# A two-layer encoder trunk on one core: the banks of a value projection, the order of the wide pools, and the last squares and output queues changed

## The chip, the cores and the metric

The kernel runs on one core of a Trainium2 chip. The metric is the device time of one execution in microseconds (us); of three runs of the kernel before, the median is 2415.16 us (2414.27 to 2418.61). The profile is of one more execution. TensorE (PE; PEld is its weight load) multiplies, VectorE (DVE) and ScalarE (ACT) do elementwise work, GpSimd (POOL) small copies and stores, and SyncE (SP) issues most DMAs. Each engine works through its own instructions in the order in which they were put there. TensorE writes to PSUM, eight banks of 128 x 512 float32.

## The reference

One sequence of 1024 frames, 1024 channels, two layers. Layer 0 projects the normed input to an RWKV-7 group and an attention group; layer 1 is a convolution module. Each layer is followed by a squared-ReLU MLP, and a last RMSNorm gives the output.

```
x = x + mixer(rmsnorm(x, g0))                      # layer 0
    p_rwkv, q, k, v = split(h @ w_in)              # 8 heads x 64 of each group
    y = concat(rwkv7(p_rwkv), band_attention(q, k, v)) @ w_out
x = x + square(relu(rmsnorm(x, g1) @ up0)) @ dn0
x = x + conformer_conv(rmsnorm(x, g2))             # pw1, GLU, width-31 conv, LayerNorm, silu, pw2
x = x + square(relu(rmsnorm(x, g3) @ up1)) @ dn1
out = rmsnorm(x, gf)
```

The RWKV-7 group keeps a 64 x 64 state for each head and updates it frame by frame. In attention each chunk of 64 frames sees itself and the eight chunks before it.

## The kernel before, in words

The 1024 frames are worked on as two halves of 512 (h = 0 and 1); activations lie as eight tiles of 128 channels x 512 frames. Each dense product is made of three passes at reduced precision: the float32 operands are split into a high and a low part (`split` for activations, `weight_part`, L258 and L259, for weights: ACT casts the high part `wh`, DVE subtracts it to get the low part `wl`), and `dense` (L144) multiplies high by high, low by high and high by low. `gemm` runs over output tiles, loads the weights for each (L250, on SP's queue, four raw buffers `wr`), sums over eight k in a PSUM bank, and hands the bank to an `evac` function.

The first part of the program has these banks: d=2 for dense work, w=2, v=1 and c=1 for the recurrence, a=2 for attention. It projects half 0 (`w_in_gemm(0)`), then runs `rwkv(0)` and `attention(0)` while `w_in_gemm(1)` projects half 1, then `rwkv(1)` and `attention(1)` beside the output projection (`mixer_out(0)`, which reads the results of recurrence and attention, yd) and the MLP of half 0. Priorities set the order: instructions of the recurrence come before those of attention, and these before dense ones, which are put where nothing else is ready; dense matmuls come in runs (6 or 12) that are not broken up.

At the end of `w_in_gemm` the value projection (L422 to L437) computes V with frames on partitions: four banks, one for each 128 frames, all four fed by the same weight part for each k. There are four buffers for split weights here (pool wp1). The four banks are d, d, a, a (`SPARE`), for both halves. ACT scales each bank by the frames' norm factor and POOL's queue stores it to vd, which attention loads.

The recurrence uses w for its products, v to transpose and invert (L676, L688, L705), and c (`keep["cb"]`, L449) for the chain over chunks and the end of a unit (L736 to L784). Attention uses its two a banks for scores (L861, L863), transposed probabilities (L883) and the output product (visit helper, L160).

From L1159 on the program is in its wide part: five d banks, two output tiles at a time, eight split weight buffers. Its pools take the memory that the first part's pools (LoRA weights, wp1, middle tiles mp, recurrence, attention) give back: wp2 (weights), mp2 (middle tiles), sx, and up (conv weights dwt, halo, conv tiles), each above the one before. A tile in memory used earlier waits until the earlier tiles there are read.

At the very end the last MLP of half 1 adds its down projection to x (L913). Its last two output tiles are computed in two column halves of 256 frames. For each tile ACT squares x (L220), DVE adds the square to the sum `acc` (L221), ACT scales by gf (L1053), TensorE transposes (L1059) and ACT and DVE copy the result to output tiles (L1065, L1067). After the last tile of a column half, `write` sums `acc` over channels by a product with ones (L1079), takes the root and the reciprocal (L1082, L1083), scales four output tiles (ACT two, DVE two) and issues their four DMAs on SP (L1092).

Of the kernel before, what the change touches and what calls it, by code (L numbers as in the profile page):

```python
# [11 lines left out]
ALU = mybir.AluOpType  # L12
# [52 lines left out]
def encoder_trunk(ctx: ExitStack, tc: tile.TileContext, x, vecs, consts, ext, w2a2, g2, w_in, w_out,  # L65
# [108 lines left out]
    def boost():  # L174
        return At("support")
# [224 lines left out]
    def w_in_gemm(h, rhs, st, first=()):  # L400
        def evac(m, q, cols):
            rstd = st.rstd()
            s = tmp("t1")
            if Q0 <= m < K0:
                nc.vector.scalar_tensor_tensor(out=s[:], in0=q[:], scalar=0.125, in1=rstd[:],
                                               op0=ALU.mult, op1=ALU.mult)
            else:
                nc.vector.tensor_tensor(out=s[:], in0=q[:], in1=rstd[:], op=ALU.mult)  # L408
            ts = slice(h * T, (h + 1) * T)
            if Q0 <= m < V0:  # L410
                hi = tmp("t2")
                nc.scalar.copy(hi[:].bitcast(F32R), s[:])
                nc.vector.tensor_tensor(out=s[:].bitcast(F32R), in0=s[:], in1=hi[:], op=ALU.subtract)
                nc.gpsimd.dma_start(ph[m][:, ts], hi[:])
                stored[h, m] = nc.gpsimd.dma_start(pl[m][:, ts], s[:])
            else:
                stored[h, m] = nc.gpsimd.dma_start(pd[m][:, ts], s[:])

        run_of(RUN[0])
        gemm(w_in, 0, IN_ORDER, rhs, evac, st, first, mark=h)  # L420
        run_of(RUN[2])
        qs = [psum(tag) for tag in SPARE]  # L422
        for k in range(KT):
            with boost():
                hi, lo = (a[:].rearrange("p a b -> p (a b)")
                          for a in weight_part(w_in[k * P : (k + 1) * P, V0 * P : V0 * P + RW], RW))
            xh, xl = rhs[k]
            for t, q in enumerate(qs):
                ts = slice(t * P, (t + 1) * P)
                dense(q[:], xh[:, ts], hi, start=(k == 0), stop=False)  # L430
                dense(q[:], xl[:, ts], hi, start=False, stop=False)
                dense(q[:], xh[:, ts], lo, start=False, stop=(k == KT - 1))
        with boost():
            for t, q in enumerate(qs):
                s = tmp("t1")
                nc.scalar.activation(s[:], q[:], AF.Copy, scale=st.part[1][:, t : t + 1])
                nc.gpsimd.dma_start(vd[h * T + t * P : h * T + (t + 1) * P, :], s[:])  # L437
# [481 lines left out]

        gemm(w, row0, range(KT), rhs, evac, taper=taper, after=after, halves=halves)  # L920

    def norm_collect(xs, gname):
        st = Stat()
        rhs = [None] * KT

        def last(m, cols):
            if gname is not None:
                rhs[m] = split(xs[m][:], m, v(gname, m))
            st.add(xs[m][:], cols)

        return st, rhs, last

# [9 lines left out]
        return nrhs, st  # L942

    def ffn(xs, rhs, rst, up, dn, mp, nxt, out_to=None, late=None):
        st, nrhs, last = norm_collect(xs, nxt)
        if out_to is not None:
            out_to.st = st
        groups = DFF // D
        mids = [[None] * KT for _ in range(groups)]
        ahead = 2 if wide[0] else 0  # L950

        def evac(m, q, cols):
            rstd = rst.rstd()
            t = tmp("t1")
            nc.vector.scalar_tensor_tensor(out=t[:], in0=q[:], scalar=0.0, in1=rstd[:], op0=ALU.max, op1=ALU.mult)  # L955
            sq = tmp("t2")
            nc.scalar.activation(sq[:], t[:], AF.Square)  # L957
            hi = mp.tile([P, T], F32R, tag="mh", name="mh")
            nc.scalar.activation(hi[:], t[:], AF.Square)  # L959
            lo = mp.tile([P, T], F32R, tag="ml", name="ml")  # L960
            nc.vector.tensor_tensor(out=lo[:], in0=sq[:], in1=hi[:].bitcast(F32), op=ALU.subtract)  # L961
            mids[m // KT][m % KT] = (hi, lo)

        done = 0
        for grp in range(groups):
            end = grp == groups - 1
            if late is not None and end:
                with At("mixer"):
                    late()
            upto = min((grp + 1) * KT + ahead, DFF // P)  # L970
            gemm(up, 0, range(done, upto), rhs, evac, rst)
            done = upto
            residual_gemm(dn, grp * D, mids[grp], xs, last=last if end else None, taper=end and nxt is None,
                          after=out_to.add if end and out_to is not None else None,
                          halves=out_to is not None and out_to.final)
        return nrhs, st
# [68 lines left out]
    class Out:  # L1045
# [5 lines left out]
        def add(self, m, cols):  # L1051
            n = tmp("t1")
            nc.scalar.activation(n[:, cols], self.xs[m][:, cols], AF.Copy, scale=v("gf", m))  # L1053
            q = psum("o")
            c2, j = divmod(m, 4)
            ts = range(cols.start // P, cols.stop // P)
            for t in ts:
                with At("dense"):
                    nc.tensor.transpose(q[:, t * P : (t + 1) * P], n[:, t * P : (t + 1) * P], ident)  # L1059
            for t in ts:  # L1060
                if self.o[4 * c2 + t] is None:
                    self.o[4 * c2 + t] = self.op.tile([P, T + TAPS - 1], F32, tag="u", name="u", bufs=8)
                dst, src = self.o[4 * c2 + t][:, j * P : (j + 1) * P], q[:, t * P : (t + 1) * P]
                if t % 2:
                    nc.vector.tensor_copy(dst, src)  # L1065
                else:
                    nc.scalar.copy(dst, src)  # L1067
            if self.final and m == KT - 1:
                self.write(ts)

        def finish(self):
            with boost():
                self.write(range(4))

        def write(self, ts):
            q = psum("o")
            for t in ts:
                with At("dense"):
                    nc.tensor.matmul(q[:, t : t + 1], self.st.acc[:, t * P : (t + 1) * P], ones[:, 0:1], start=True, stop=True)  # L1079
            w = slice(ts[0], ts[-1] + 1)  # L1080
            r = self.r
            nc.scalar.activation(r[:, w], q[:, w], AF.Sqrt, bias=kc[:, 0:1], scale=1.0 / D)  # L1082
            nc.vector.reciprocal(out=r[:, w], in_=r[:, w])  # L1083
            for c2 in range(2):
                for t in ts:
                    rows = slice(self.h * T + t * P, self.h * T + (t + 1) * P)
                    o = self.o[4 * c2 + t][:, 0:T]
                    if t % 2:
                        nc.scalar.activation(o, o, AF.Copy, scale=r[:, t : t + 1])
                    else:  # L1090
                        nc.vector.tensor_scalar(o, o, r[:, t : t + 1], None, op0=ALU.mult)
                    nc.sync.dma_start(out[rows, c2 * T : (c2 + 1) * T], o)  # L1092


    with banks(d=2, w=2, v=1, c=1, a=2), tc.tile_pool(name="lop", bufs=1) as lop, tc.tile_pool(name="wp1", bufs=4) as wb[0]:
# [62 lines left out]

    wide[0] = True  # L1159
    run_of(1)  # L1160
    with banks(d=5, w=1, o=2), tc.tile_pool(name="wp2", bufs=8, reuse_waits="tile") as wb[0], tc.tile_pool(name="mp2", bufs=10, reuse_waits="tile") as mp, tc.tile_pool(name="sx", bufs=4, reuse_waits="tile") as extra[0], tc.tile_pool(name="up", bufs=1, reuse_waits="tile") as up:
        dwt = up.tile([P, KT * TAPS], F32, tag="dwt", name="dwt")
        nc.scalar.dma_start(dwt[:], vecs[:, VOFF["dw"] : NVEC])
        halo = up.tile([P, KT, TAPS - 1], F32, tag="halo", name="halo")
        nc.gpsimd.memset(halo[:], 0.0)
        us = glu(0, r, s, up)
        with At("mixer"):
            ca, sca = conv(us, up)
        with boost():
            xb = fetch_x(1)  # L1170
        r, s = mixer_out(1, xb, mp)
        r, s = ffn(xb, r, s, up0, dn0, mp, "g2", late=lambda: conv_norm(ca, sca, up))
        stash_x(1, xb)
        us = glu(1, r, s, up)
        with boost():
            xa = fetch_x(0)
        r, s = pw2_block(ca, xa)
        with At("mixer"):
            cb, scb = conv(us, up)
        o = Out(0, xa, up, False)  # L1180
        ffn(xa, r, s, up1, dn1, mp, None, o, late=lambda: conv_norm(cb, scb, up))
        deferred.append(o.finish)
        with boost():
            xb = fetch_x(1)
        r, s = pw2_block(cb, xb)
        ffn(xb, r, s, up1, dn1, mp, None, Out(1, xb, up, True))
        deferred.pop()()
# [69 lines left out]
```

## Time and profile before

| | us |
|---|---|
| median of three runs | 2415.16 |
| profiled execution | 2409.59 |
| its span, first to last instruction | 2407.5 |
| TensorE busy | 2374.8 |
| DVE busy | 1706.2 |
| ACT busy | 1198.9 |
| POOL busy | 117.1 |

A row of the timeline has the start in us, the duration in us, engine, line, operation, output tile <- input tiles, shapes and a count of merged instructions; in brackets stands how long the engine was idle before it and which work ended that wait. A row for a stretch has its bounds, its length, the busy time of PE, PEld, DVE, ACT and POOL with their instruction counts, the granted TensorE clock as a share of full speed, the share of the 16 DMA engines that was busy, and GB/s. Matmuls overlap: one shows 0.39 us, but they start about 0.23 us apart.

### The profile page before, as it was taken

The numbers are of one execution on the slowest core, as the hardware profiler recorded it, in microseconds if no ns is written. First come the engines' busy times: TensorE is split into PE (matmuls) and PEld (weight loads), VectorE is DVE, ScalarE is ACT, GpSimd is POOL, SyncE is SP. The second block draws the span as 40 slices with busy tenths as digits, with TensorE's granted clock in tenths as the row PEclk, the third lists the DMA queues.
The fourth block names the chain that finished last, engine by engine and source line by source line (L and its number), as shares of the span: only waits on it lengthen the run. The fifth ranks groups of instructions, "written<-read, shape, count | busy, mean of one in ns | idle before, by whom it ended". The sixth has DMA issues, their size and how long they took to land.

```text
span 2407.5 us, 37122 instructions
## 1 busy us (share of the span) xinstructions
PE 2374.8 (99%) x12804; PEld 1956.4 (81%) x12804; DVE 1706.2 (71%) x3575; ACT 1198.9 (50%) x2323; POOL 117.1 (5%) x243
## 2 busy tenths in 40 slices
PE   9999999899999999999999999999999999999998
PEld 7777777788888888888888888888888888888887
DVE  6787776587777764579999746799997465434434
ACT  6567666677676753434433335334333365423324
POOL 1120111100000000011000000000000000000000
PEclk9999999999999999999999999999999999999999
DMA  8574445633343323453333334433333334333332
GB/s 260 163 217 139 120 121 171 188 102 115 93 120 110 90 74 90 145 166 92 101 97 97 97 97 135 123 94 97 96 98 99 95 112 140 97 97 97 97 98 67
DMA packets 476042, 283.34 MB, mean 118 GB/s; under 512 B 44512, under 2 KB 453216, under 8 KB 475856
## 3 DMA queue, kind: packets, MB, share of 16 engines
q1 hardware_dynamic: 464976, 249.46, 35.7%
q0 software_dynamic: 9488, 30.28, 3.6%
q8 instruction: 101, 1.65, 0.3%
q10 hardware_dynamic: 1392, 1.24, 0.2%
q14 instruction: 85, 0.70, 0.1%
HBM read 247.31 MB, written 36.72 MB: 118 GB/s over the span
## 4 chain that ended last, share of the span: by engine, by line
PE 88%; DVE 4%; DMA 3%; ACT 3%; issue 1%; SPq 1%; ACTq 0%; DVEq 0%
PE d L144 77%; DMA pt<-pd 1%; PE a L160 1%; PE v L688 1%; PE a L883 1%; DVE wl L259 1%; PE a L144 1%; ACT wh L258 1%; PE a L861 1%; PE a L863 1%; PE c L746 1%; PE c L740 0%; DVE pr L650 0%; PE c L736 0%; PE v L676 0%
## 5 line engine op out<-in xcount | busy, mean ns | idle before, releaser
L258 ACT CAST wh<-wr 128x512 fp32r<-128x512 f32 x744 | 460.1, 620 | 922.9 <-PE d L144 839.0
L144 PE MATMUL d<-xh,wh 128*128 128x512 f32 x1872 | 745.6, 398 | 0.3 <-DVE t L408 0.2
L144 PE MATMUL d<-xh,wl 128*128 128x512 f32 x1872 | 730.7, 391 | 0.9 <-DVE wl L259 0.9
L144 PE MATMUL d<-xl,wh 128*128 128x512 f32 x1872 | 730.2, 390 | 0.0
L259 DVE TENSOR_TENSOR wl<-wr,wh 128x512 fp32r<-128x512 f32 x744 | 503.4, 687 | 197.5 <-ACT wh L258 142.2
L144 PEld LDWEIGHTS d<-xh,wl 128*128 128x128 f32 x1872 | 351.7, 188 | 76.4 <-DVE wl L259 1.3
L144 PEld LDWEIGHTS d<-xh,wh 128*128 128x128 f32 x1872 | 352.2, 188 | 70.0 <-issue 1.2
L144 PEld LDWEIGHTS d<-xl,wh 128*128 128x128 f32 x1872 | 352.3, 188 | 67.7 <-issue 0.5
L144 PE MATMUL d<-mh,wh 128*128 128x512 f32 (+1 forms) x1040 | 405.8, 390 | 0.0
L144 PE MATMUL d<-mh,wl 128*128 128x512 f32 (+1 forms) x1040 | 401.8, 386 | 0.0
L144 PE MATMUL d<-ml,wh 128*128 128x512 f32 (+1 forms) x1040 | 401.6, 386 | 0.0
L1014 DVE SCALAR_TENSOR_TENSOR cv<-u,dwt,cv 128x512 f32<-128x512 f32 x480 | 332.7, 749 | 0.7
L144 PEld LDWEIGHTS d<-mh,wl 128*128 128x128 f32 x1040 | 195.4, 188 | 40.0
L144 PEld LDWEIGHTS d<-ml,wh 128*128 128x128 f32 x1040 | 195.6, 188 | 37.6
L144 PEld LDWEIGHTS d<-mh,wh 128*128 128x128 f32 x1040 | 195.5, 188 | 37.7
L913 DVE TENSOR_TENSOR x<-d,x 128x512 f32<-128x512 f32 (+1 forms) x146 | 97.8, 681 | 152.1 <-PE d L144 151.6
L955 DVE SCALAR_TENSOR_TENSOR t<-d,rstd 128x512 f32<-128x512 f32 x128 | 86.6, 688 | 114.6 <-PE d L144 111.9
L961 DVE TENSOR_TENSOR ml<-t,mh 128x512 fp32r<-128x512 f32 x128 | 87.9, 689 | 12.6 <-ACT mh L959 9.5
L957 ACT ACTIVATE t<-t 128x512 f32<-128x512 f32 x128 | 80.0, 625 | 12.2 <-DVE t L955 11.2
L959 ACT ACTIVATE mh<-t 128x512 fp32r<-128x512 f32 x128 | 78.9, 616 | 0.0
L745 ACT ACTIVATE sd<-vs,dc 64x64 f32<-64x64 f32 x128 | 44.1, 345 | 40.7 <-DVE vs L749 29.6
L221 DVE TENSOR_TENSOR acc<-acc,t 128x512 f32<-128x512 f32 (+1 forms) x86 | 58.0, 675 | 8.4 <-ACT t L220 8.3
(271 smaller groups left out, 2335.0 us busy)
## 6 DMA issues: line engine op xcount, KB each, us to landing
wr<-in_up_dram SPq DMA_DIRECT2D x256, 256.0 KB
wr<-in_dn_dram SPq DMA_DIRECT2D x256, 256.0 KB
wr<-in_w_in_dram SPq DMA_DIRECT2D x103, 256.0 KB
wr<-in_pw_dram SPq DMA_DIRECT2D x96, 256.0 KB
wr<-in_w_out_dram SPq DMA_DIRECT2D x32, 256.0 KB
pd<-t POOLq DMA_DIRECT2D x28, 256.0 KB, 2.6
x<-xd SPq DMA_DIRECT2D x24, 256.0 KB
pt<-pd SPq DMA_DIRECT2D x42, 128.5 KB
```

The source lines that it names most:

```text
L144: ins = nc.tensor.matmul(*a, **k)
L160: ins = issue(*a, **k)
L221: nc.vector.tensor_tensor(out=self.acc[:, cols], in0=self.acc[:, cols], in1=sq[:, cols], op=ALU.add)
L258: nc.scalar.copy(hi[:], raw[:])
L259: nc.vector.tensor_tensor(out=lo[:], in0=raw[:], in1=hi[:].bitcast(F32), op=ALU.subtract)
L745: nc.scalar.activation(sd[hs[hd], :], sv[hs[hd], hd, c, :], AF.Copy, scale=dc[hs[hd], c : c + 1])
L913: nc.vector.tensor_tensor(out=xs[m][:, cols], in0=q[:, cols], in1=xs[m][:, cols], op=ALU.add)
L955: nc.vector.scalar_tensor_tensor(out=t[:], in0=q[:], scalar=0.0, in1=rstd[:], op0=ALU.max, op1=ALU.mult)
L957: nc.scalar.activation(sq[:], t[:], AF.Square)
L959: nc.scalar.activation(hi[:], t[:], AF.Square)
L961: nc.vector.tensor_tensor(out=lo[:], in0=sq[:], in1=hi[:].bitcast(F32), op=ALU.subtract)
L1014: nc.vector.scalar_tensor_tensor(out=c[:], in0=u[:, tap : tap + T], scalar=dw(tap), in1=c[:], op0=ALU.mult, op1=ALU.add)
```

## The change

Three edits. The value projection of half 1 takes the banks d, d, v, c; half 0's stays. The pools of the wide part are opened in the order up, mp2, sx, wp2. At the end of half 1, the squares of the last tile are computed by DVE and not added to `acc`: the product with ones sums `acc` and the squares in one PSUM group (twice as many small matmuls) and stands ahead of the last transposes. There ACT scales one of the four output tiles in place of two, and the second and third DMA of each column half are issued on ACT's queue. The output of half 0 keeps its way, in a function cut in two.

```
-        qs = [psum(tag) for tag in SPARE]
+        qs = [psum(tag) for tag in (SPARE if h == 0 else ("d", "d", "v", "c"))]
...
-    def norm_collect(xs, gname):
+    def norm_collect(xs, gname, final=False):
...
-            st.add(xs[m][:], cols)
+            if final and m == KT - 1:
+                sq = tmp("t2")
+                nc.vector.tensor_tensor(out=sq[:, cols], in0=xs[m][:, cols], in1=xs[m][:, cols], op=ALU.mult)
+                st.rest = sq
+            else:
+                st.add(xs[m][:], cols)
...
-        st, nrhs, last = norm_collect(xs, nxt)
+        st, nrhs, last = norm_collect(xs, nxt, out_to is not None and out_to.final)
...
-            q = psum("o")
             c2, j = divmod(m, 4)
             ts = range(cols.start // P, cols.stop // P)
+            if self.final and m == KT - 1:
+                self.sums([self.st.acc, self.st.rest], ts)
+            q = psum("o")
...
+        def sums(self, parts, ts):
             q = psum("o")
+            pairs = [(part, t) for part in parts for t in ts]
+            for i, (part, t) in enumerate(pairs):
                 with At("dense"):
+                    nc.tensor.matmul(q[:, t : t + 1], part[:, t * P : (t + 1) * P], ones[:, 0:1],
+                                     start=(i == 0), stop=(i == len(pairs) - 1))
             w = slice(ts[0], ts[-1] + 1)
             r = self.r
             nc.scalar.activation(r[:, w], q[:, w], AF.Sqrt, bias=kc[:, 0:1], scale=1.0 / D)
             nc.vector.reciprocal(out=r[:, w], in_=r[:, w])
...
+        def write(self, ts):
+            r = self.r
+            for i, (c2, t) in enumerate((c2, t) for c2 in range(2) for t in ts):
+                rows = slice(self.h * T + t * P, self.h * T + (t + 1) * P)
+                o = self.o[4 * c2 + t][:, 0:T]
+                if i == 1 if self.final else t % 2:
+                    nc.scalar.activation(o, o, AF.Copy, scale=r[:, t : t + 1])
+                else:
+                    nc.vector.tensor_scalar(o, o, r[:, t : t + 1], None, op0=ALU.mult)
+                queue = nc.scalar if self.final and i in (1, 2) else nc.sync
+                queue.dma_start(out[rows, c2 * T : (c2 + 1) * T], o)
...
-    with banks(d=5, w=1, o=2), (pools) wp2, mp2, sx, up:
+    with banks(d=5, w=1, o=2), (pools) up, mp2, sx, wp2:
```

The last two lines are shortened to the pools' names; their sizes are unchanged.

More of the change, by code (lines that the diff above doesn't have):

```diff
@@ L1069, in add @@
                 self.write(ts)
[L1071 to L1075, printed above, removed]
+        def sums(self, parts, ts):
             q = psum("o")
-            for t in ts:
+            pairs = [(part, t) for part in parts for t in ts]
+            for i, (part, t) in enumerate(pairs):
                 with At("dense"):
-                    nc.tensor.matmul(q[:, t : t + 1], self.st.acc[:, t * P : (t + 1) * P], ones[:, 0:1], start=True, stop=True)
+                    nc.tensor.matmul(q[:, t : t + 1], part[:, t * P : (t + 1) * P], ones[:, 0:1],
+                                     start=(i == 0), stop=(i == len(pairs) - 1))
             w = slice(ts[0], ts[-1] + 1)
@@ L1083, in write, with finish @@
             nc.vector.reciprocal(out=r[:, w], in_=r[:, w])
[L1084 to L1092, printed above, removed]
+        def finish(self):
+            with boost():
+                self.sums([self.st.acc], range(4))
+                self.write(range(4))
+        def write(self, ts):
[9 more added lines that the diff above has]
+                queue.dma_start(out[rows, c2 * T : (c2 + 1) * T], o)
     with banks(d=2, w=2, v=1, c=1, a=2), tc.tile_pool(name="lop", bufs=1) as lop, tc.tile_pool(name="wp1", bufs=4) as wb[0]:
@@ L1160, in encoder_trunk @@
     run_of(1)
-    with banks(d=5, w=1, o=2), tc.tile_pool(name="wp2", bufs=8, reuse_waits="tile") as wb[0], tc.tile_pool(name="mp2", bufs=10, reuse_waits="tile") as mp, tc.tile_pool(name="sx", bufs=4, reuse_waits="tile") as extra[0], tc.tile_pool(name="up", bufs=1, reuse_waits="tile") as up:
+    with banks(d=5, w=1, o=2), tc.tile_pool(name="up", bufs=1, reuse_waits="tile") as up, tc.tile_pool(name="mp2", bufs=10, reuse_waits="tile") as mp, tc.tile_pool(name="sx", bufs=4, reuse_waits="tile") as extra[0], tc.tile_pool(name="wp2", bufs=8, reuse_waits="tile") as wb[0]:
         dwt = up.tile([P, KT * TAPS], F32, tag="dwt", name="dwt")
```

## The prediction

> **What bounds the kernel now.** I read the page's totals first, then the busy table of chosen stretches, then the order of instructions at the three places that the change touches.
>
> ```profile
> span 2407.5 us, 37122 instructions
> PE 2374.8 (99%) x12804; PEld 1956.4 (81%) x12804; DVE 1706.2 (71%) x3575; ACT 1198.9 (50%) x2323; POOL 117.1 (5%) x243
> ```
>
> The stretches (length, busy time of each engine, granted clock, DMA share, GB/s):
>
> ```profile
> core 0: us, PE busy (x) PEld busy (x) DVE busy (x) ACT busy (x) POOL busy (x), PEclk, DMA share, GB/s
> 110.00:440.00 330.00, 318.83 (x2353) 255.33 (x2352) 246.26 (x746) 219.78 (x510) 47.77 (x103) 0.99 0.53 158
> 475.00:945.00 470.00, 466.51 (x3227) 384.88 (x3227) 338.87 (x978) 312.09 (x655) 15.46 (x42) 1.00 0.35 100
> 429.49:464.50 35.01, 29.67 (x147) 23.11 (x146) 16.96 (x39) 21.66 (x43) 4.80 (x15) 0.95 0.57 182
> 435.50:446.00 10.50, 5.88 (x45) 4.09 (x44) 2.21 (x10) 4.39 (x9) 0.54 (x1) 0.89 0.41 146
> 446.00:457.00 11.00, 11.00 (x47) 9.10 (x48) 7.37 (x15) 6.71 (x13) 2.44 (x7) 0.95 0.52 161
> 457.00:459.50 2.50, 1.78 (x9) 1.13 (x8) 2.16 (x6) 2.45 (x7) 0.29 (x2) 1.00 0.91 292
> 1025.00:1035.00 10.00, 9.07 (x40) 7.16 (x40) 7.39 (x12) 5.50 (x10) 0.54 (x1) 1.00 0.90 274
> 2403.25:2405.75 2.50, 0.00 (x0) 0.00 (x0) 0.00 (x0) 0.00 (x0) 0.00 (x0) 0.50 1.00 381
> ```
>
> TensorE is busy 2374.8 of 2407.5 us, so 32.7 us is all that it leaves idle, and the change takes no dense matmul away: it can only fill idle time, restore the clock, or shorten the end. The rows say where that lies. The 35 us from the first V matmul of half 1 (429.49) to the first matmul behind the projection (464.50) hold 35.01 - 29.67 = 5.34 us of idle time, 4.62 of it from 435.5 to 446. The move to the wide pools holds 0.93 (1025 to 1035). The 470 us in which half 1's recurrence and attention run beside dense work hold 3.49, 0.7%; the same mixture for half 0 holds 11.17 in 330, 3.4%. The last row is the output write: all 16 DMA engines full at 381 GB/s.
>
> **Part 1, V projection of half 1 in banks d, d, v, c.** The order now:
>
> ```profile
> 427.78 0.42 DVE L784 TENSOR_TENSOR e<-e,c 128x256 f32<-128x256 f32 x1
> 429.49 0.39 PE L144 MATMUL d<-wh,xh 128*128 128x512 f32 x1
> 435.25 0.40 PE L144 MATMUL d<-wl,xh 128*128 128x512 f32 x1
> 435.49 0.49 PE L883 MATMUL a<-cst,pt 128*128 128x128 f32 x3
> 441.89 1.27 PE L883 MATMUL a<-cst,pt 128*128 128x128 f32 x8 [3.32 <-ACT pt L874]
> 443.88 1.97 PE L160 MATMUL a<-pT,vt 128*64 128x128 f32 x16 [0.73 <-ACT pT L884]
> 445.79 0.80 PE L144 MATMUL a<-wh,xh 128*128 128x512 f32 x1
> 445.91 0.29 DVE L894 COPY yo<-a 128x128 f32<-128x128 f32 x1 [4.49 <-PE a L160]
> 447.82 0.62 ACT L258 CAST wh<-wr 128x512 fp32r<-128x512 f32 x1 [3.99 <-PE a L144]
> 449.76 0.37 SPq L938 DMA_DIRECT2D mh<-yd  x1
> 464.28 0.39 PE L144 MATMUL a<-wl,xh 128*128 128x512 f32 x1
> ```
>
> The d matmuls of the first four k run up to 435.25; there the four weight buffers are full, because the a matmuls of the same k must wait until attention of half 0 gives up both score banks (L160 at 443.88 is its last use, the first V matmul in a starts at 445.79). So the last softmax of attention stands alone, and TensorE waits 3.32 and 0.73 us in it. The cast of the fifth weight part waits until 447.82, and with it the raw buffer and everything behind it on SP's queue, the recurrence's loads for half 1 among it.
>
> In v and c no such wait is in sight: the recurrence of half 0 reads c for the last time at 427.78 to 428.20, before V begins. V's 96 matmuls can then run from 429.49 without a break, and attention's steps slip between them; its softmax is what V now hides. That removes 4.62 us of idle time. The granted clock adds to it: 0.11 x 5.88 busy us in one row and 0.05 x 11.00 in the next, 0.65 + 0.55 = 1.2 us. [...]
>
> At most, then, 5.34 + 1.2 = 6.5 us. I take 5.3: the 0.72 at 457 to 459.5 is a wait for the recurrence's first product (LoRA), which is not V's and comes along, and 0.5 is kept for attention's steps that now wait behind runs of six dense matmuls. From below: if attention's end rather than V's sets the start of the next projection, 2 us (second rival). Moved with V are four more weight loads and their casts ahead of 447, and the stores of V on POOL's queue: all earlier, with DMA at 0.41 in that stretch. The added waits: the recurrence of half 1 needs v and c after V's evacuation (four ACT copies behind V, by about 464). Its first use of v, and its last step of all (the latest of the 16):
>
> ```profile
> 481.80 0.55 PE L705 MATMUL v<-cst,bk 128*128 128x128 f32 x3
> ```
>
> ```profile
> L784 DVE TENSOR_TENSOR e<-e,c x16: 401/420/422, 163.7 to 956.6; 128x256 f32<-128x256 f32 x16
> ```
>
> Its loads come up to 13 us earlier now, so that use moves to about 468, still later. Were it to wait, only the recurrence would stand behind it, and that ends at 957, 69 us before the wide pools begin, with dense work to fill TensorE: the price is nothing.
>
> **Part 2, pool order.** At the move the trace shows this:
>
> ```profile
> 1023.04 1.28 ACT L258 CAST wh<-wr 128x512 fp32r<-128x512 f32 x2
> 1026.63 0.39 PE L144 MATMUL d<-xl,wh 128*128 128x512 f32 x1
> 1027.21 1.28 DVE L259 TENSOR_TENSOR wl<-wr,wh 128x512 fp32r<-128x512 f32 x2
> 1027.95 0.50 PE L144 MATMUL d<-xh,wl 128*128 128x512 f32 x1 [0.93 <-DVE wl L259]
> ```
>
> The high half of the first wide weights is ready at 1024, the low half is computed only at 1027.21. By the order of the pools the wide weights come to lie first, over the weights and middle tiles of the last down projection, which are read until then. In the new order the conv pool lies there (first written well after), and the weights lie far up, over what recurrence and attention of half 1 left by 957. The low halves then follow their casts at about 1024. The step from 1026.63 to 1027.95 is 1.32 us, where a step between neighbours is 0.24 (435.25 to 435.49): gain 1.1. Bounds: 1.3 with the slow step behind it; minus 1 if a tile of another pool now waits as the low half did. The conv weights' load sits on ACT's queue: it waits for a LoRA tile, dead long before.
>
> **Part 3, the end.** The last half tile runs so:
>
> ```profile
> 2393.61 0.50 PE L1079 MATMUL o<-ones,acc 128*128 128x1 f32 x4
> 2396.22 0.42 ACT L220 ACTIVATE t<-x 128x256 f32<-128x256 f32 x1 [0.23 <-DVE x L913]
> 2399.00 0.42 DVE L913 TENSOR_TENSOR x<-d,x 128x256 f32<-128x256 f32 x1 [0.84 <-PE d L144]
> 2399.52 0.42 ACT L220 ACTIVATE t<-x 128x256 f32<-128x256 f32 x1 [1.69 <-DVE x L913]
> 2399.97 0.43 DVE L221 TENSOR_TENSOR acc<-acc,t 128x256 f32<-128x256 f32 x1 [0.54 <-ACT t L220]
> 2400.66 0.50 PE L1079 MATMUL o<-ones,acc 128*128 128x1 f32 x4
> 2401.16 0.29 DVE L1065 COPY u<-o 128x128 f32<-128x128 f32 x1 [0.77 <-ACT u L1067]
> 2401.20 0.26 ACT L1082 ACTIVATE orst<-o,small 128x2 f32<-128x2 f32 x1
> 2401.70 0.88 DVE L1091 TENSOR_SCALAR u<-u,orst 128x512 f32<-128x512 f32 x2
> 2402.21 0.81 SPq L1092 DMA_DIRECT2D out_dram<-u  x2
> ```
>
> The output's issues, shortest, median and longest in ns:
>
> ```profile
> L1092 SPq DMA_DIRECT2D out_dram<-u x16: 333/412/603, 2008.0 to 2403.6; - x16
> ```
>
> Now: add, ACT square, DVE sum, transposes, sums at 2400.66, root 2401.20, first scale 2401.70. After: DVE squares right behind the add, 2399.44 to 2399.87 (0.43 as L221), and the sums on it start at 2399.92. With the rows' own spacing (sums to root 0.54, root to scale 0.50) the first scale stands at 2400.96, 0.74 earlier. If the DVE copy of the last transpose, which waits for ACT's copy and that for the root, stays ahead of it, it is 0.37. I take 0.55. The write's 1 MB fills the DMA engines from the first issue on, so the end moves with the first issue, and a second queue that saves parts of 0.41 us of issuing adds nothing that I count (bounds 0 to 0.2). [...]
>
> The first column half pays: four more small matmuls in front of dense work, 0.50 us for four with their start-up, about 0.09 each when they follow one another, so 0.35. ACT also issues two of its four DMAs there, the second behind a DVE scale; queued behind it is the square at 2396.22, which two issues of 0.41 just clear (bounds 0 to 0.3). Net: 0.55 - 0.35 = 0.2, from -0.3 to 0.9.
>
> **Sum.** 5.3 + 1.1 + 0.2 = 6.6 us. The profiled execution took 2409.59 (span 2407.5 and 2.1 around it), so its like would take 2403.0. That execution lies 5.6 below the median of 2415.16; I carry the difference over: 2415.16 - 6.6 = 2408.6. What an experiment can tell from no change here is about 0.2%, 4.8 us; the forecast lies a little beyond it.
>
> **Rivals.** First, slower: the whole of half 1 is put in a new order. Its recurrence starts some 13 us earlier, while V, the next projection's casts and attention's loads still run, and its steps stand on TensorE's in-order queue ahead of dense work. Where they wait, dense work waits. For it: the two waits behind V already are of this kind, and half 0, where everything starts together, loses 3.4%. Against it: half 1 loses 0.7% in the same code. At half 0's rate 470 us would lose 15.9 instead of 3.5, 12.4 more: 2408.6 + 12.4 = 2421.0. It decides from an idle share of about 2.1% (6.6 us over 470). Chance 0.08.
>
> Second: the gap moves. The next projection reads attention's last tile at its eighth k. Attention's last product (443.88 to 445.85) came at once on an idle TensorE; between runs of six (1.4 us), some six steps could cost it up to 8 us, so 454. From its end to the load of that tile on SP lie 3.9 us (445.85 to 449.76, the copy at 445.91 and a store between); with some 2 for load and split, my estimate, that is 460. V ends about 429.49 + 29 = 458.5, and 21 matmuls of a first unit cover up to 463. Little is left over; if 3 us reappear there the gain is 3.6, 2411.6. Chance 0.18.
>
> Third: the change doesn't do what it says in V, because the bank c or v is handed over later in the new order than the 428.20 of now, or attention's steps still come in one block. Then parts 2 and 3 are left, 1.3 us: 2413.9. Chance 0.09.
>
> Fourth: half 1's remaining idle time shrinks as well, since SP's queue no longer stands still up to 447: 3 us more, 2405.6. Chance 0.10.
>
> **How the numbers follow.** The forecast keeps 0.55, over gains of about 5 to 8. Faster by over 0.2% (below 2410.3): 0.55 + 0.10 = 0.65. Within: 0.18 + 0.09 = 0.27. Slower than before: 0.08, the first rival; at its price it is just over 0.2%. Below, part 1 at 6.5 and the end at 0.9 give 2406.7, and most of the fourth rival's 3 us lead to 2404.5; above, the range takes in the second and third rival with some room and reaches to no change, 2415.5; outside lie the first rival and little else.
>
> **What would show it.** Right: V matmuls into d, v and c without a gap between about 429 and 452, no wait of attention's L883 above 1 us, clock 1.00 from 435 to 457, the dense work behind V starting near 459; the low halves of the first wide weights computed near 1024 and no TensorE wait at 1026; the root about 0.7 us after the squares, and the output's rate unchanged at about 381 GB/s. Wrong: a gap of 3 us or more between V and the next projection; idle time from 475 to 945 above 10 us; the first output issue less than 0.3 us closer to the last dense matmul.

## The result, and the profile after

| us | median | lowest to highest | runs |
|---|---|---|---|
| before | 2415.95 | 2414.27 to 2418.61 | 4 |
| after | 2433.95 | 2430.46 to 2436.71 | 4 |

The ratio is 1.0073, with an interval of 1.0055 to 1.0090: the change makes the kernel 18 us slower. The forecast was 2408.6, faster. The profiled execution of after took 2430.46 us. The medians below leave out three executions that took 3934, 7287 (both of before) and 4190 us (e5). The totals of after's profile:

```profile
span 2428.6 us, 37101 instructions
PE 2396.8 (99%) x12812; PEld 1956.1 (81%) x12812; DVE 1711.9 (70%) x3577; ACT 1193.9 (49%) x2319; POOL 108.5 (4%) x243
```

The span is 21.1 us longer than before, and TensorE is busy 22.0 us longer (2396.8 against 2374.8), with eight more matmuls, all small. Its idle time, 31.8 us against 32.7, is as it was. So no new wait made the kernel slower: TensorE takes longer over the same products. The groups of instructions by line show which ones. Before (count, then busy us, mean ns of one):

```profile
L144 PE MATMUL d<-xh,wl 128*128 128x512 f32 x1872 | 730.7, 391 | 0.9 <-DVE wl L259 0.9
L144 PE MATMUL d<-xl,wh 128*128 128x512 f32 x1872 | 730.2, 390 | 0.0
...
L144 PE MATMUL d<-mh,wl 128*128 128x512 f32 (+1 forms) x1040 | 401.8, 386 | 0.0
```

After:

```profile
L144 PE MATMUL d<-xh,wl 128*128 128x512 f32 x1872 | 739.8, 395 | 0.0
L144 PE MATMUL d<-xl,wh 128*128 128x512 f32 x1872 | 737.1, 394 | 0.0
...
L144 PE MATMUL d<-mh,wl 128*128 128x512 f32 (+1 forms) x1040 | 401.8, 386 | 0.0
```

Two of the three products of the normed activations (xh, xl) grew by 9.1 and 6.9 us at the same count, and the third, xh by wh, by 5.0 (745.6 to 750.6); those of the middle tiles (mh), with weights from the same buffers, did not grow. What takes the place of the stretches of before, in the table of chosen stretches of after (length, busy time of each engine, granted clock, DMA share, GB/s):

```profile
428.91:455.91 27.00, 27.00 (x144) 21.23 (x142) 14.03 (x32) 18.29 (x35) 4.77 (x12) 1.00 0.60 187
455.91:1027.46 571.55, 561.07 (x3662) 462.48 (x3661) 394.03 (x1072) 360.98 (x744) 22.38 (x59) 0.99 0.38 110
1027.46:2428.62 1401.16, 1394.42 (x6177) 1138.79 (x6175) 985.73 (x1571) 533.16 (x919) 19.44 (x33) 1.00 0.34 102
475.00:945.00 470.00, 462.35 (x3191) 381.61 (x3190) 335.67 (x971) 307.88 (x644) 15.52 (x42) 0.99 0.35 99
2424.35:2426.85 2.50, 0.00 (x0) 0.00 (x0) 0.00 (x0) 0.00 (x0) 0.00 (x0) 0.70 1.02 380
```

The first three are the program from the first V matmul of half 1 to the end, cut at the next projection's first matmul and at the first of the wide part. The same cuts of before, whose first stretch is the 35.01 us from 429.49:

```profile
464.50:1026.40 561.90, 557.48 (x3657) 460.06 (x3656) 388.08 (x1059) 356.21 (x732) 24.00 (x64) 1.00 0.38 108
1026.40:2407.45 1381.05, 1372.39 (x6169) 1137.84 (x6167) 982.92 (x1574) 539.43 (x927) 26.62 (x25) 1.00 0.35 104
```

V went from 35.0 to 27.0 us and lost all its idle time, as forecast. The stretch behind it grew from 561.9 to 571.55, and its idle time from 4.42 to 10.48. Both together: 596.9 before, 598.55 after; their idle time 9.76 and 10.48. What V gained was given back in these two executions. And the wide part, which was to gain 1.3, grew from 1381.05 to 1401.16, by 20.1 us: there lies the result.

**Behind V.** The timeline of after, cut to what TensorE waits for:

```profile
455.68 0.39 PE L144 MATMUL c<-wl,xh 128*128 128x512 f32 x1
455.91 0.39 PE L144 MATMUL d<-xh,wh 128*128 128x512 f32 x1
...
461.18 0.69 ACT L436 ACTIVATE t<-v,rc 128x512 f32<-128x512 f32 x1 [2.43 <-DMA vd<-t]
461.76 0.39 ACT L524 CAST xl<-e 64x256 fp32r<-64x256 f32 x1
...
462.19 0.42 DVE L525 TENSOR_TENSOR xl<-e,xl 64x256 fp32r<-64x256 f32 x1 [2.92 <-ACT xl L524]
...
462.66 0.39 PE L543 MATMUL w<-xl,lora 128*128 128x256 f32 x1 [1.15 <-DVE xl L525]
...
464.68 0.39 PE L543 MATMUL w<-xl,lora 128*128 128x256 f32 x1 [1.52 <-DVE xl L525]
```

The next projection follows V without a gap (455.68, 455.91). Five microseconds on, the recurrence of half 1 opens (L543), and TensorE stands 1.15 and 1.52 us for its LoRA input. Read upwards: the product waits for DVE, DVE for the cast on ACT, and the cast is queued behind ACT's third evacuation of V, which waited 2.43 us for a store of V to leave its buffer. Before, the same product came while V was still running:

```profile
458.26 0.39 PE L543 MATMUL w<-xl,lora 128*128 128x256 f32 x1 [0.72 <-DVE xl L525]
```

Counted from V's first matmul that is 28.8 us (458.26 - 429.49), and after it is 33.8 (462.66 - 428.91), although V itself had become 8 us shorter. In after, the recurrence's loads on SP's queue, and the store of attention's last tile of half 0 on POOL's:

```profile
433.88 18.27 SPq L250 DMA_DIRECT2D wr<-in_w_out_dram  x6
452.32 0.38 SPq L943 DMA_DIRECT2D mh<-yd  x1
452.76 0.90 SPq L482 DMA_DIRECT2D pt<-pd  x2
449.63 0.54 POOL L895 DMA_DIRECT2D yd<-yo  x1 [8.69 <-DVE yo L894]
```

The loads (`pt`) are issued at 452.76; before, the first was issued at 451.07. V ended 8.6 us earlier and the loads no earlier. Ahead of them on the queue stand six weight loads, the last issued at 451.79, and the load of attention's last tile (`mh<-yd`), which needs the store of 449.63. That store went out at 446.49 before: attention, with its steps between V's, ended 3.1 us later than when it had TensorE to itself. Whether the weight loads or attention's end held the recurrence's loads was not tried.

**At the move to the wide pools**, in the timeline of after:

```profile
1023.58 1.37 ACT L258 CAST wh<-wr 128x512 fp32r<-128x512 f32 x2 [1.10 <-DMA wr<-in_pw_dram]
...
1024.23 1.45 DVE L259 TENSOR_TENSOR wl<-wr,wh 128x512 fp32r<-128x512 f32 x2 [1.03 <-ACT wh L258]
...
1027.69 0.40 PE L144 MATMUL d<-xl,wh 128*128 128x512 f32 x1
...
1027.92 0.39 PE L144 MATMUL d<-xh,wl 128*128 128x512 f32 x1
```

The low halves follow their casts at 1024.23, and the step that took 1.32 us takes 0.23 (1027.69 to 1027.92).

**At the end:**

```profile
2420.39 0.28 PE L144 MATMUL d<-mh,wl 128*128 128x256 f32 x1
...
2420.71 0.42 DVE L913 TENSOR_TENSOR x<-d,x 128x256 f32<-128x256 f32 x1 [0.24 <-PE d L144]
2421.17 0.42 DVE L931 TENSOR_TENSOR t<-x 128x256 f32<-128x256 f32 x1
...
2421.65 0.61 PE L1083 MATMUL o<-ones,t 128*128 128x1 f32 x4 [0.64 <-DVE t L931]
...
2422.29 0.26 ACT L1087 ACTIVATE orst<-o,small 128x2 f32<-128x2 f32 x1 [0.61 <-PE o L1083]
...
2422.78 0.49 DVE L1103 TENSOR_SCALAR u<-u,orst 128x512 f32<-128x512 f32 x1
...
2423.34 1.29 SPq L1105 DMA_DIRECT2D out_dram<-u  x2
...
2423.54 0.83 ACTq L1105 DMA_DIRECT2D out_dram<-u  x2
```

From the last dense matmul to the first output issue: 2.95 us (2420.39 to 2423.34). Before it started at 2398.68, and the first issue at 2402.21: 3.53. The end came nearer by 0.54 (8.77 to 8.23 us), and the write runs at 380 GB/s (before 381).

### The profile page after: what moved, and what is told of

Same layout as the page of the kernel before. It is cut to its first block, busy times and chain, and to the rows that moved or that the text cites. A ratio compares the mean times of both kernels' runs of the same rounds, so it can differ in the third digit from the quotient of the medians.

```text
span 2428.6 us, 37101 instructions
## 1 busy us (share of the span) xinstructions
PE 2396.8 (99%) x12812; PEld 1956.1 (81%) x12812; DVE 1711.9 (70%) x3577; ACT 1193.9 (49%) x2319; POOL 108.5 (4%) x243
## 4 chain that ended last, share of the span: by engine, by line
PE 83%; DVE 4%; DMA 4%; issue 4%; ACT 3%; SPq 1%; POOL 0%; DVEq 0%; ACTq 0%; POOLq 0%
PE d L144 74%; DMA pt<-pd 1%; DVE wl L259 1%; PE v L688 1%; DMA nb<-msc 1%; PE a L160 1%; PE a L144 1%; PE a L883 1%; ACT wh L258 1%; PE a L861 0%; PE c L740 0%; DMA vd<-t 0%; PE c L746 0%; PE a L863 0%; PE v L676 0%
## 5 line engine op out<-in xcount | busy, mean ns | idle before, releaser
L144 PE MATMUL d<-xh,wh 128*128 128x512 f32 x1872 | 750.6, 401 | 0.3
L144 PE MATMUL d<-xh,wl 128*128 128x512 f32 x1872 | 739.8, 395 | 0.0
```

What stands on the lines that cost most here:

```text
L144: ins = nc.tensor.matmul(*a, **k)
```

## The experiments

The line that tells most is in the code, not in the profile: `LINE = 32` and `whole(n)`, which rounds a row of a tile up to 32 floats, 128 bytes; "line" below is this constant of the code. Other tiles of odd size go through it; those of the conv pool `up` do not (`dwt` 992 bytes a partition, `halo` 960, `u` 2168). In the compiled kernel before, the operands of all wide products start at a multiple of 128 bytes, and `up` lies above them. In after `up` lies lowest, its rows take 992 and 960 bytes and eight times 2176, and every pool above it starts 32 bytes past a multiple of 128: the wide weights, the middle tiles, and the two normed tiles in sx (k = 0 and 1). The other six normed tiles (k = 2 to 7) lie in a pool that the change does not touch, on a multiple.

The theory, drawn from these places and from the rows by line above, and put to the test below: TensorE takes longer over a product when its weights and its moving tile start at different distances past a multiple of 128 bytes. Rivals: the pool order itself (what lies over what, and its waits), the banks of V, or the end. A time without an interval is a single execution. A ratio, with its 95% interval, is taken over the executions and need not be the quotient of the two medians. The start of V of half 1 lay between 426.6 and 437.7 us in these profiles, also where the instructions up to it are the same, so stretches are compared from there on.

**e1_after_whole_lines.** After, with the conv tiles rounded to whole lines:

```diff
-        dwt = up.tile([P, KT * TAPS], F32, tag="dwt", name="dwt")
+        dwt = up.tile([P, whole(KT * TAPS)], F32, tag="dwt", name="dwt")
...
-        halo = up.tile([P, KT, TAPS - 1], F32, tag="halo", name="halo")
+        halo = up.tile([P, KT, whole(TAPS - 1)], F32, tag="halo", name="halo")
...
-                u = up.tile([P, T + TAPS - 1], F32, tag="u", name="u", bufs=8)
+                u = up.tile([P, whole(T + TAPS - 1)], F32, tag="u", name="u", bufs=8)
```

> The changed kernel, with the tiles of the conv pool (conv weights 992 bytes, halo 960, conv input 2168 per partition) widened to whole 128-byte lines, so that the pools opened after it start on a line again; order of pools, banks and end unchanged. Line theory (the wide matmuls are slow because weights start 32 bytes past a line while the normed activations start on one): steps of the up projections go back from 231-237 to 227 ns, the wide part from 1401 to about 1380 us, total about 2413 to 2415. Place theory (the weights lie far up, away from the activations): steps and total stay, about 2434. Theory of the banks (what was lost came with the value projection): stays near 2434.

Measured: 2410.07 against 2415.59, ratio 0.9983 (0.9969 to 0.9996). The loss is gone, with order, banks and end all as in after.

**e2_pools_only.** Before, with the new pool order alone (the edit of the diff's last two lines).

> The kernel before with the new order of the wide pools alone. Line and place theory: the wide part 20 us longer, the wait of 1.3 us at the move gone, about 2416 + 20 - 1 = 2435. Theory of the banks: 2415.

Measured: 2435.58 against 2415.59, ratio 1.0078 (1.0061 to 1.0095): the whole loss comes with part 2.

**e3_before_shift_32 and e7_before_shift_64.** Before, in the old order, with a small tile ahead of the wide pools, written once; 8 floats, or 16 in e7:

```diff
-    with banks(d=5, w=1, o=2), (pools) wp2, mp2, sx, up:
+    with banks(d=5, w=1, o=2), (pools) shift, wp2, mp2, sx, up:
+        nc.gpsimd.memset(shift.tile([P, 8], F32, tag="shift", name="shift")[:], 0.0)
```

> The kernel before, pools in the old order, with a 32-byte tile (written once, never read) ahead of them, so that all wide pools start 32 bytes past a line. Line theory: up-projection steps 231 to 237 ns, about 2416 + 20 = 2436. Place theory: no change, 2416.

> The kernel before with a 64-byte tile ahead of the wide pools. If the unit is 128 bytes: up-projection steps at 231 to 237 ns as with 32 bytes, 20 us more. If it is 64 bytes: 227 ns, no change.

Measured: e3 2437.03 against 2415.59, ratio 1.0079 (1.0059 to 1.0098); e7, a single execution, 2428.87, with 2414.2 as median of before beside it. A pad of 32 bytes, which moves no work at all, costs what the change costs. 64 bytes cost as much: from the first wide matmul to the end e3 takes 1400.96 us and e7 1400.65, where before takes 1381.05. The total of e7 is lower because its V began at 426.55 us and that of e3 at 434.96. A distance of 64 bytes was therefore not free either.

**e6_moving_shift_32.** The same tile of 8 floats, but between wp2 and mp2: the weights stay on a multiple, the middle tiles and sx come to lie 32 bytes past one.

> The kernel before with the 32-byte tile behind the wide weights: weights on a line, middle activations (and the first two normed tiles) 32 bytes past one. If what counts is that weights and moving tile differ in their place within a line, the down projections' steps rise from 227 to 231-237 ns (some 2240 wide steps, 5 to 7 ns each: 11 to 16 us), and the up projections' stay at 227 for six of eight k. If only weights off a line cost: nothing, 227 everywhere.

Measured, a single execution: 2435.58 beside 2414.2, and 1403.52 from the first wide matmul to the end. The loss is there again, but in other products. It is seen best in two neighbouring stretches of 192 products each, from the first matmul of a kind to the first of the other: first an up projection (normed tiles), then a down projection (middle tiles). Before, then after, then e1 (up alone), e3, e6 and e7 (up alone):

```profile
1258.94:1302.46 43.52, 43.52 (x193) 36.05 (x192) 43.48 (x69) 16.25 (x29) 2.41 (x2) 1.00 0.33 98
1302.46:1345.98 43.52, 43.52 (x193) 36.05 (x192) 43.19 (x68) 12.17 (x21) 1.20 (x1) 1.00 0.33 97
```

```profile
1263.86:1308.52 44.66, 44.66 (x194) 36.05 (x192) 44.24 (x70) 16.25 (x29) 2.41 (x2) 1.00 0.32 95
1308.52:1352.08 43.56, 43.56 (x194) 36.04 (x193) 43.12 (x67) 12.12 (x21) 1.21 (x1) 1.00 0.33 97
```

```profile
1266.25:1309.77 43.52, 43.52 (x194) 36.04 (x192) 43.45 (x69) 16.26 (x29) 2.40 (x2) 1.00 0.33 98
```

```profile
1270.87:1315.43 44.56, 44.56 (x194) 36.06 (x192) 44.17 (x70) 16.27 (x29) 2.40 (x2) 1.00 0.33 95
1315.43:1358.97 43.54, 43.54 (x193) 36.05 (x192) 43.15 (x67) 12.14 (x21) 1.20 (x1) 1.00 0.33 97
```

```profile
1264.74:1308.73 43.99, 43.99 (x193) 36.02 (x192) 43.45 (x70) 16.26 (x29) 1.80 (x2) 1.00 0.33 96
1308.73:1353.54 44.81, 44.81 (x194) 35.98 (x192) 43.87 (x68) 12.17 (x21) 1.20 (x1) 1.00 0.32 94
```

```profile
1263.34:1307.87 44.53, 44.53 (x193) 35.94 (x192) 44.16 (x70) 16.23 (x29) 2.40 (x2) 1.00 0.32 95
```

In all of them TensorE is busy without a gap at full granted clock (1.00), so the length is the number of products times the step. Set beside the places of the operands, in bytes past a multiple of 128:

| | weights | moving tiles | step, ns (length / 192) |
|---|---|---|---|
| before, up and down | 0 | 0 | 226.7 |
| after, down | 32 | 32 | 226.9 |
| after and e3, up | 32 | 0 (k = 0, 1: 32) | 232.6 and 232.1 |
| e6, down | 0 | 32 | 233.4 |
| e6, up | 0 | 0 (k = 0, 1: 32) | 229.1 |
| e7, up | 64 | 0 (k = 0, 1: 64) | 231.9 |

Neither operand had to start on a multiple of 128: with both 32 bytes past one the step was 226.9 ns, against 226.7 with both on it. What the two rows without a loss share is that both operands lie at the same place; with 32 bytes between them in all eight k or in six the step was 232.1 to 233.4. The mixed rows agree: in after six k of eight are apart, and 1.14 us over their 144 products is 7.9 ns for each; in e7 the same six, 64 bytes apart, and 1.01 over 144 is 7.0; in e6 two of eight, and 0.47 us over 48 is 9.8; in e6's down projection all, 1.29 over 192, 6.7. Whether 128 bytes is the distance that counts these runs do not show: wherever a product lost nothing, its two operands lay a multiple of 512 bytes apart, and 128 or 256 bytes were not tried. One more rival is in these rows: DVE, which splits the weights, is busy 43.48 of 43.52 us before, so a slower DVE would slow everything. In the slow stretch of e6 it has 0.94 us to spare (43.87 of 44.81), and the split writes the same weight buffers in both stretches of e3, of which only one is slow. It is not DVE.

**e4_banks_only.** Before, with the V banks d, d, v, c alone.

> The kernel before with the banks d, d, v, c for the value projection of half 1 alone. If the changed kernel's traces are read rightly, V ends some 8.6 us earlier and the stretch from there to the wide part is some 9.7 us longer: total 2416 + 1 = 2417, within 0.2%. By my prediction's first term alone: 2411.

Measured: 2410.25 against 2415.59, ratio 0.9983 (0.9968 to 0.9997), 4.1 us faster (0.7 to 7.7). The expected 2417 did not come; the total is what the prediction's first term alone would give. In the profile V and the stretch behind it take 26.95 + 568.46 = 595.41 us, only 1.5 less than before.

**e10_whole_lines_old_banks and e11_whole_lines_again.** e1 with `SPARE` for both halves, so parts 2 and 3 alone; and e1 once more, on the same chip.

> The changed kernel on whole lines with the old banks d, d, a, a for both halves: pool order and end alone. By the traces the move saves 1.1 us and the end 0.6: from the wide part's first matmul to the end 1379.2 in place of 1381.0, total 1.8 us below before, ratio 0.9993. If the banks of V bring nothing at all, the ratio equals that of the first experiment, 0.9983.

> The first experiment once more, on the same chip as the two others, as their measure: ratio to before 0.998, V's first matmul to the wide part 597.

Measured: e10 2411.49, ratio 0.9992 (0.9983 to 1.0001); e11 2411.15, ratio 0.9991 (0.9982 to 1.0000). e10 came as expected; e11 missed both numbers, its ratio and the 597 us, in whose place it took 598.85. By this pair the V banks are worth 0.3 us, by the ratio of e1 less 1.9 us for parts 2 and 3 some 2, by e4 some 4: part 1 brings something between nothing and 4 us, and only e4 separates it, barely, from nothing. The profiles agree: from V's first matmul to the wide part the old banks take 596.9 to 601.5 us (before, e2, e3, e6, e7, e10) and the new ones 595.4 to 598.9 (after, e1, e4, e11); the means are 1.7 us apart, and the ranges overlap. The stretches of e1 and e10 (V, from there to the wide part, the rest):

```profile
437.74:464.75 27.01, 27.01 (x144) 21.23 (x142) 14.04 (x32) 18.29 (x35) 4.75 (x12) 1.00 0.59 186
464.75:1034.93 570.18, 560.64 (x3662) 462.50 (x3660) 393.74 (x1072) 360.97 (x745) 22.29 (x60) 0.99 0.38 111
1034.93:2414.07 1379.14, 1372.51 (x6177) 1138.42 (x6175) 979.31 (x1571) 534.70 (x919) 28.98 (x33) 1.00 0.35 103
```

```profile
432.54:468.09 35.55, 30.94 (x147) 24.02 (x146) 17.08 (x39) 21.66 (x43) 4.71 (x15) 0.90 0.55 178
468.09:1031.46 563.37, 557.79 (x3658) 460.18 (x3656) 390.56 (x1065) 358.79 (x737) 22.22 (x56) 1.00 0.38 109
1031.46:2410.60 1379.14, 1372.53 (x6177) 1138.57 (x6175) 979.63 (x1571) 534.85 (x919) 29.29 (x34) 1.00 0.35 103
```

The wide part is 1379.14 in both, 1.9 less than before: parts 2 and 3, once the lines are right. Idle time from V to the wide part: 4.61 + 5.58 = 10.19 us with the old banks, 0 + 9.54 with the new, and 11.27 in the repeat e11. The new banks take it out of V, and it comes back behind V, to within about a microsecond. The time of both stretches is 598.9 us in e10, 597.2 in e1 and 598.85 in e11.

**e5_whole_lines_v_four_buffers.** e1, with four buffers in place of two for V's evacuation, to take away ACT's wait of 2.43 us:

```diff
-                s = tmp("t1")
+                s = tmp("t1" if t < 2 else "t2")
```

> The changed kernel on whole lines (as the first experiment), with V's four evacuations in four temporary buffers instead of two. In the changed kernel's trace the third evacuation on ACT waits 2.4 us for a store of V to land, and behind it on ACT stand a cast of the recurrence, then TensorE's product of it (1.2 + 1.5 us idle) and all dense work. Store theory (V's gain of 8.6 us is given back in this wait): those two idle times go, and the stretch from V's end to the wide part shrinks from about 570 to about 566 us. Order theory (it is given back because the recurrence's loads stand behind weight loads on SP's queue and begin no earlier than before, so that V no longer covers the start of half 1): the stretch keeps at least 568 us, the idle time only moves.

Measured: 2410.77 against 2414.2, ratio 0.9985 (0.9974 to 0.9997). It decides nothing: the edit changed TensorE's order from half 0 on, and V took 32.5 us with 2.98 idle in it, so the wait was not tried alone.

**e8_whole_lines_loads_on_pool.** e1, with the recurrence's two first loads of half 1 off SP's queue:

```diff
-                nc.sync.dma_start(t[:, 0 : RT + 1], pd[ct][:, t0 - 1 : t0 + RT])
+                queue = nc.gpsimd if tb == 2 and ct in (12, 13) else nc.sync
+                queue.dma_start(t[:, 0 : RT + 1], pd[ct][:, t0 - 1 : t0 + RT])
```

> The changed kernel on whole lines, with the first two loads of half 1's recurrence on POOL's queue instead of SP's, where they stand behind six weight loads until 452. Order theory: the recurrence of half 1 starts up to 20 us earlier, under V, its first products no longer hold TensorE up, and the stretch from V's first matmul to the wide part shrinks from 597 to about 592 us; total about 4 us below the first experiment. Store theory: ACT's wait for V's stores stays and with it the idle time, no change.

Measured: 2405.66 against 2414.2, ratio 0.9966 (0.9953 to 0.9979), the fastest of all and 4.4 us below e1, as the order theory had it. But not in the way that was meant. The two loads, in the view by tile (shortest, median and longest issue in ns, first and last start in us):

```profile
L483 POOL DMA_DIRECT2D pt<-pd x2: 541/542/543, 451.5 to 452.0; - x2
```

They are still issued at 451.5, so SP's queue was not all that held them: on POOL's queue they stand behind the store of attention's last tile, issued at 449.49. V with the stretch behind it takes 596.3 us (597.2 in e1, 598.85 in e11) and not 592, with 9.76 of it idle. Between the two profiled executions most of the difference lies ahead of V, which began at 428.77 us in e8 and at 437.74 in e1, and there both kernels have the same instructions in the same order. What of the lower median the edit brought was not found; that the total met the expectation is luck as far as the profile shows.

**e9_half1_opens_later.** e1, with the recurrence's first products of half 1 (L543) held back to the third tile of the output projection, after 60 dense matmuls behind V in place of 24:

```diff
+        if h == 0:
+            for ins in opening:
+                tc.add_manual_dep(ins.ins, marks["mix", 2].ins.name,
+                                  mybir.DependencyInfo(mybir.DependencyClass.NoSync, mybir.DependencyReason.DATA),
+                                  reason="half 1 opens behind the first tiles of the output projection")
```

> The changed kernel on whole lines, with the recurrence's first products of half 1 (LoRA, four matmuls) put on TensorE behind 60 dense matmuls of the output projection instead of 24. In-order theory (V's gain is given back because TensorE comes to these products before their inputs exist, and dense work stands behind them): the two idle times of 1.2 and 1.5 us after V go, the first 74 us behind V hold some 3 us less idle time (6 to 3), V's first matmul to the wide part shrinks from 597 to about 593, total about 4 us below the first experiment. Rival (the recurrence's and attention's start costs TensorE the same wherever it stands): the idle time moves on by some 8 us and stays at 6.

Measured: 2410.46 against 2413.64, ratio 0.9987 (0.9977 to 0.9997), no better than e11 beside it. TensorE's waits in the 80 us from 455 (what waited, for what: us in total, times, longest):

```profile
PE d L238 <- ACT rc L231: 2.2, 1, 2.2
PE a L863 <- DMA kk<-pl: 1.4, 1, 1.4
PE a L885 <- ACT pt L876: 1.0, 1, 1.0
PE d L144 <- ACT rstd L240: 0.7, 1, 0.7
```

The waits of L543 are gone and four others stand there. From V to the wide part TensorE idles 10.98 us, where e1 idles 9.54 and e11 11.27. As the rival had it, the idle time moved on and stayed.

## Why the prediction was wrong, point by point

**The step that failed** is the sentence that the change takes no dense matmul away and so "can only fill idle time, restore the clock, or shorten the end", and with it part 2's bounds, +1.3 to minus 1. It treated the duration of a matmul as given and priced the new pool order by its waits alone. The order also sets where every tile above the first pool starts, and the conv pool's 992 + 960 bytes put the wide weights 32 bytes off the normed tiles. e2 shows the loss with the order alone, e3 shows it with 32 bytes and no new order, e1 takes it away with the order kept. From the wide part's start to the end after takes 1401.16 us and e1 1379.14: 22.0 us for the 32 bytes. With it, the forecast's 2408.6 would have been 2430.6, and with part 1 at 1.7 in place of 5.3 (below) 2434.2; measured was 2433.95. No rival held it; the slower case that I priced was one of waits. None of the three signs that the text named for being wrong appeared: none of them looked at how long a product takes.

**Part 1, 5.3 us.** V lost its 5.34 us of idle time and got its clock back (1.00 for 0.95), as worked out. It was worth 0 to 4 us in the end, 1.7 by the means of the profiles. The total took it for granted that what follows V would be ready sooner as well. The text had the recurrence's loads up to 13 us earlier; they came 1.7 us later. So the recurrence's first product, which had come inside V, now came 7 us behind it, and TensorE reached it before its input existed (waits of 1.15 and 1.52 us), with the rest of the dense work behind it in its order. This is argued from the rows behind V; e5 and e8, which were to take it apart, did not. In effect it is the second rival (the gap moves), with a price of 3.6 us by those means where the rival had 3, but at another place. Attention did end later, by 3.1 us. For the load and split of its last tile the rival had some 2 us, an estimate that no row showed; in after they took 6.5, from the issue at 452.32 to the end of the split at 458.84 (DVE, 458.15 and 0.69). Yet the next projection, which the rival had waiting for it, followed V without a gap, and reached its eighth k, which reads that tile, at 460.67; what TensorE waited for was the start of half 1's recurrence. e9 shows that it is not one step which can be put off; the idle time went on to the next.

**The first rival**, 12.4 us of idle time in half 1's recurrence, did not come: 475 to 945 holds 7.65 idle where it held 3.49, below the 10 that the text set.

**Part 2's wait, 1.1 us**: 1.09. **Part 3, at the end 0.55**: 0.54. That is partly luck: 0.55 lay halfway between two cases of 0.74 and 0.37. The DVE copy did not stay ahead of the first scale (2423.19 and 2422.78), which is the case of 0.74, and the root came 0.64 us behind the sums (2421.65 to 2422.29) and not 0.54. The price of 0.35 in the first column half did not show: the wide part of e10 is 1.91 us shorter than before's, and 1.09 + 0.54 = 1.63 would leave no room for it. The second queue saved nothing that the end shows, as forecast: all issues were in by 2424.6, and the write ran at 380 GB/s.

**Open:** what holds the recurrence's loads when V ends earlier (weight loads and attention's end both stand ahead of them), what part 1 is worth between nothing and 4 us, and what e8 gained beyond e1.

## What to carry to other kernels

When pools are put in another order or a tile changes its size, work out where every tile behind it starts, and compare the place of a matmul's weights with that of its moving tile; round odd tiles up, or put them last. Here a multiple of 512 bytes between the two was free (226.7 and 226.9 ns a step), and 32 and 64 bytes were not (232.1 to 233.4 ns with 32 bytes in six or all of eight k, 231.9 with 64 in six). When busy time of the bounding engine grows at an unchanged count, look at the mean of one instruction by its operands before looking for a wait. And when a gap on the bounding engine is filled, look whether the work behind it can start sooner too: here the recurrence's loads did not (452.76 us against 451.07), and the idle time from V to the wide part was 9.76 us before, 5.34 of it in V, and 10.48 after, none of it in V.

## What the runs showed of the hardware

One matmul step of 128x128 weights and 128x512 moving elements, in the three-pass float32 products of this kernel, took 226.7 to 226.9 ns here when its two operands lay a multiple of 512 bytes apart, whether both started on a multiple of 128 or both 32 bytes past one. It took 6.7 to 9.8 ns more when they lay 32 bytes off that, with either operand on the multiple (after and e6), and 7.0 ns more at 64 bytes (44.53 us for 192 products in e7, of which 144 were apart, 43.52 before). Other distances were not tried, 128 and 256 among them, and neither was a size at which the cost would end. Why the place matters no run shows. TensorE's busy share stays at 100% and the granted clock at 1.00 in the slow stretches, so neither shows it; only the mean of one instruction and the count in a stretch of fixed length do.
